# MLP of a hybrid decoder trunk: the low parts that GpSimd made are made by VectorE

## The chip, the cores and the metric

The kernel runs on one core of one Trainium2 chip. A core has five engines with a queue of instructions each: TensorE (PE in the profile; its weight loads are PEld), VectorE (DVE), ScalarE (ACT), GpSimd (POOL) and SyncE (SP), which here only issues DMAs. Each engine works its queue in order and waits for the others through semaphores. The metric is the time of one execution on the device, in microseconds (us); lower is better. Times given for a kernel are medians of several runs, and beside them stands one execution that was profiled.

## The reference

One decoder layer in float32 on 2048 tokens of width 1024: a mixer (retention and pooling), cross-attention into 256 memory tokens, and a gated MLP, each behind an RMSNorm and with a residual, and a last RMSNorm. The change lies in the MLP, whose inner width D_FF is 2816:

```python
def conv_glu_ffn(h, w_up, conv_w, conv_b, w_down):
    a = h @ w_up
    S = a.shape[1]
    a1 = jnp.pad(a, ((0, 0), (1, 0), (0, 0)))[:, :S]
    a2 = jnp.pad(a, ((0, 0), (2, 0), (0, 0)))[:, :S]
    c = conv_w[0] * a2 + conv_w[1] * a1 + conv_w[2] * a + conv_b
    gate, val = jnp.split(c, 2, axis=-1)
    return (jax.nn.silu(gate) * val) @ w_down
...
x = x + conv_glu_ffn(rmsnorm(x, ffn_norm_g[l]), ffn_w_up[l], ffn_conv_w[l],
                     ffn_conv_b[l], ffn_w_down[l])
return rmsnorm(x, final_norm_g)
```

## The kernel before

**Numbers in two parts.** Activations stand with features on the 128 partitions and tokens along the free axis. A float32 operand x of a matrix product is kept as a high part hi, x rounded to the type that TensorE multiplies at full rate (fp32r), and a low part lo = x - hi. A product is then three matmuls into one PSUM bank, hi by hi, hi by lo and lo by hi (`passes`, L241 to L243).

**Seven products for eight.** Each matrix product of the MLP is cut into 2 x 2 blocks, of the weights (two column blocks by two halves of the inner dimension) and of the tokens (two halves of 512 tokens by the same two halves), and done in seven block products in the manner of Strassen and Winograd. They need sums of weight blocks and of token blocks. Sums of weight blocks are made long before by accumulating DMAs and lie in DRAM (`Ud`, `Dd`). Sums of token blocks are made by GpSimd (`sums_of`, in four tensor operations on 128 x 512) and stored to DRAM (`Hd`, `Gd`) through SyncE's queue (`send`).

**Rounds.** The 2048 tokens are two batch halves b of 1024. `rounds` lists eight rounds: the up-projection of half 0 and of half 1, 22 members (`Up`) each, and then for each half the down-projection in three rounds of 4 members (`Down`), over 3, 4 and 4 tiles of the inner dimension. A member is one pair of column blocks of weights with its seven products i = 0 to 6; a product with n inner tiles is 3n matmuls, 12 in the up rounds. Up members run one by one, apart from the first two and the last two, which alternate product by product; down members alternate in pairs.

**Combined tokens.** A round needs 7n tiles of combined tokens, `right(i, j)`, each a high and a low part of 128 x 512 in the tensor G. `combining` makes one: a load from DRAM into a slot T (L948), the high part on ScalarE (L955; L953 for the negated product 2), the low part by `low`, or by one instruction on VectorE for product 2. Tiles for the next round are begun as soon as the last product of the running round that uses their place is done, so they come in a burst where two rounds meet.

**Weights.** For each product of a member the block is loaded into a slot R (L1000), ScalarE writes its high part (L1006) and `low` its low part into one of seven pair buffers, three in the tensor Q and four in G. They are made up to seven products ahead of TensorE.

**How a low part is made.** `low` (L934) has three ways: `""`, one subtraction on VectorE with both inputs in SBUF; `"copy"`, in which ScalarE first copies x to PSUM (tile `aux`, L940) and VectorE subtracts from there; and `"pool"`, the same subtraction on GpSimd. A member's `how` names one for each product: in `Up` products 2 and 6 go the pool way, in `Down` products 2 and 6 too. Of the combined tokens every fourth goes the pool way (`rd.shared`), in the second and third round every third, apart from product 2; the others of product 1 go the copy way. All tensor-tensor operations are recorded in one helper, `tt`, at L216, and all scalar-tensor-tensor ones in `stt`, at L225; so the profile tells them apart by engine and tiles: a subtraction into G or Q, from R (weights) or T, consts and state (tokens), is a low part.

**After a product.** `evac` of `Up` copies a product's bank into Z on ScalarE (L1052) or adds it there on VectorE (`Z<-Z,mm`); products 0, 2, 4 and 6 accumulate in one bank, so the evacuation of each must be done before the next of them starts, one product later. Then come the causal convolution, a scaled copy on ScalarE (L1069) and two steps on VectorE (`Z<-Z,vecs` of 1024 columns), SiLU on ScalarE (L1081), the gating product on VectorE (`Z<-Z` of 1024 columns), its store (L974), and for each second member the token sums for the down rounds. `evac` of `Down` adds or subtracts into Z. During the up rounds of half 0 the tokens of half 1 are normalised (VectorE, `T<-T,vecs`) and summed (GpSimd).

**What sets the order.** `run` walks over all products and writes each engine's instructions in program order: low parts of pairs just begun, the matmuls, the evacuation, then the next pairs and loads, then up to two steps of convolutions, then steps of combined tiles. A scheduler in the framework then moves instructions on each engine by its own estimate of times, within the dependences. SyncE's queue carries loads and stores of the MLP alike, in that order.

Of the kernel before, what the change touches and what calls it, by code (L numbers as in the profile page):

```python
# [8 lines left out]
F32 = mybir.dt.float32  # L9
# [3 lines left out]
ALU = mybir.AluOpType  # L13
# [106 lines left out]
def trunk(ctx, tc, xT, memT, pos, w_qkgu, w_v, wkv, wqT, wo, wout_r, wout_p, poolT, w_up, w_dn, vecs, consts, outT):  # L120
    nc = tc.nc
    pe, act, dve, pool, sp = nc.tensor, nc.scalar, nc.vector, nc.gpsimd, nc.sync
# [83 lines left out]
    def aux():  # L206
        if both[0] and next(turns_) % 3 == 2:
            return single()
        return auxp.tile([P, SUB], F32, tag="aux", name=nm("aux"))
# [5 lines left out]
    def tt(eng, out, a, b, op):  # L215
        return eng.tensor_tensor(out=out, in0=a, in1=b, op=op)  # L216
# [7 lines left out]
    def stt(out, a, s, b, op0=ALU.mult, op1=ALU.add):  # L224
        dve.scalar_tensor_tensor(out=out, in0=a, scalar=s, in1=b, op0=op0, op1=op1)  # L225
# [698 lines left out]
    class Round:  # L924


        def __init__(self, src, n, groups):
            self.src, self.n, self.groups = src, n, groups

            self.shared = 4  # L930

    def right(i, j, h):
        at = (4 * i + j) * T + h * SUB
        return G[:, at : at + SUB]  # L934

    def low(x, hi, lo, how):

        if how == "copy":
            t = aux()[:, : x.shape[-1]]
            act.activation(t, x, AF.Copy)  # L940
            x = t
        tt(pool if how == "pool" else dve, lo, x, hi.bitcast(F32), ALU.subtract)

    def combining(rd, i, j):

        r = TT.take()
        x = r.f[:, :SUB]
        sp.dma_start(x, rd.src(i, j))  # L948
        yield
        yield  # L950
        hi, lo = right(i, j, 0), right(i, j, 1)
        if i == 2:
            act.activation(hi, x, AF.Copy, scale=-1.0)  # L953
        else:
            act.activation(hi, x, AF.Copy)  # L955
        yield
        if i == 2:
            stt(lo, x, -1.0, hi.bitcast(F32), ALU.mult, ALU.subtract)
        else:
            low(x, hi, lo, "pool" if (i * rd.n + j) % rd.shared == rd.shared - 1 else "copy" if i == 1 else "")  # L960
        r.free()

    def sums_of(b11, b12, b21, b22, t):
# [20 lines left out]
    def combine(rd, i):  # L984
        in_turn(combining(rd, i, j) for j in range(rd.n))

    class Member:
# [21 lines left out]
        def low(self, i, hi, lo):  # L1009
            low(self.raw[i].f[:, : self.n * P], hi, lo, self.how[i])  # L1010
            self.raw.pop(i).free()
# [14 lines left out]
    class Up(Member):  # L1026


        def __init__(self, b, f):
            super().__init__((w_up[f], w_up[f + NF]), Ud[f], 0, 4)  # L1030
            self.b, self.f, self.how = b, f, ("", "copy", "pool", "", "copy", "", "pool")
            self.c = {}

        def bank(self, i, spare):
# [87 lines left out]
    class Down(Member):  # L1122
# [2 lines left out]

        def __init__(self, b, j, at, k0, halves):
            super().__init__((w_dn[2 * j], w_dn[2 * j + 1]), Dd[at, j], k0, halves)
            self.b, self.j, self.at, self.how = b, j, at, ("copy", "copy", "pool", "copy", "copy", "", "pool")

        def bank(self, i, spare):  # L1130
            return gathered(self, i, spare)
# [179 lines left out]
    def rounds():  # L1311
        out = []
        for b in range(NB):
            ups = [Up(b, f) for f in range(NF)]
            groups = [ups[:2]] + [[u] for u in ups[2:-2]] + [ups[-2:]]
            out.append(Round(lambda i, j, b=b: Hd[b, j, i], 4, groups))
        for b in range(NB):
            for at, (k0, n) in enumerate(ROUNDS):
                ms = [Down(b, j, at, k0, n) for j in range(KT // 2)]
                out.append(Round(lambda i, j, b=b, k0=k0: Gd[b, k0 // 2 + j, i], n, [ms[:2], ms[2:]]))  # L1320
        out[1].shared = out[2].shared = 3
        return out

    def run(rds):
# [45 lines left out]
        def begin():  # L1370
            rd, i, j, _, first = tiles.pop(0)
            live.append((first, combining(rd, i, j)))
            next(live[-1][1])
# [125 lines left out]
    for b in range(NB):  # L1499
# [56 lines left out]
        if b + 1 < NB:  # L1556
            nxt = [TT.take() for _ in range(NS)]
            got = fetch_x(b + 1, 0)
        else:
            rds = rounds()  # L1560
# [166 lines left out]
```

## Time and profile before

| | us |
|---|---|
| median of 3 runs | 2502.49 (2500.76 to 2505.65) |
| profiled execution, its own time | 2506.72 |
| its span, from the first to the last instruction | 2504.9 |

| engine | busy us of the span | share |
|---|---|---|
| TensorE | 2442.7 | 98% |
| VectorE | 1666.9 | 67% |
| ScalarE | 1216.1 | 49% |
| GpSimd | 652.4 | 26% |

The mean granted clock of TensorE is 0.992. How the page is read: a line of a group gives line, engine, operation, tiles (out<-in, buffer numbers left out), the form and the number of instructions; then their busy us and the mean ns of one; then the idle us of the engine just ahead of them and what ended most of it. Busy time of an engine that is not the bottleneck costs nothing by itself, and an average over the span hides stages with different limits, so the views are asked by stage.

### The profile page before, as it was taken

To read this page: it belongs to the slowest core of one execution; us is meant where nothing else is said; L and a number is where in the kernel's file an instruction comes from. 1 tells how busy PE (TensorE), PEld (TensorE's weight loads), DVE (VectorE), ACT (ScalarE), POOL (GpSimd) and SP (SyncE) were. 2 spreads that over 40 slices of the span, in tenths; PEclk is the share of its full clock that TensorE was granted. 3 is DMA by queue.
4 is the path that set the end of the run, shared out by engine and by line. 5 is a ranking of instruction groups with operands and counts; after the bars stand their busy time and mean duration, and the time that the engine had idled before them with its cause. 6 is when DMAs were issued, how large, how long until landed. Compare 5 with 4: busy or idle time off the path is not lost.

```text
span 2504.9 us, 33172 instructions
## 1 busy us (share of the span) xinstructions
PE 2442.7 (98%) x11390; PEld 2037.7 (81%) x11390; DVE 1666.9 (67%) x2574; ACT 1216.1 (49%) x2163; POOL 652.4 (26%) x579
## 2 busy tenths in 40 slices
PE   6999999999999999999999999999999999999997
PEld 6888887788788888888887888878888887888885
DVE  8646566564635675574678776886677586867875
ACT  6333423343321223434654555665555576666663
POOL 1010122100121120030237352553335154222322
PEclk9999999999999999999999999999999999999998
DMA  8363888715766764366567564755556468768951
GB/s 318 89 168 110 244 191 233 234 40 181 227 152 145 159 158 149 111 221 220 167 205 270 166 203 153 236 192 165 160 160 213 136 220 287 250 185 280 346 164 68
DMA packets 257177, 474.28 MB, mean 189 GB/s; under 512 B 26864, under 2 KB 56176, under 8 KB 257008
## 3 DMA queue, kind: packets, MB, share of 16 engines
q1 hardware_dynamic: 212336, 408.18, 49.0%
q0 software_dynamic: 19584, 34.61, 8.9%
q10 hardware_dynamic: 25088, 29.37, 3.4%
q8 instruction: 89, 1.46, 0.2%
q14 instruction: 80, 0.66, 0.1%
HBM read 370.87 MB, written 170.39 MB: 216 GB/s over the span
## 4 chain that ended last, share of the span: by engine, by line
PE 78%; DMA 8%; DVE 6%; issue 3%; POOL 2%; ACT 2%; SPq 0%; POOLq 0%; ACTq 0%; DVEq 0%
PE mm L241 25%; PE mm L242 24%; PE mm L243 24%; POOL T L216 1%; DVE Z L216 1%; DMA T<-Xd 1%; DVE Z L225 1%; DVE G L216 1%; DMA T<-xT 1%; DVE Q L216 1%; DVE T L216 1%; DMA T<-Gd 1%; POOL Z L216 1%; PE aux L749 1%; DMA R<-VWd 0%
## 5 line engine op out<-in xcount | busy, mean ns | idle before, releaser
L241 PE MATMUL mm<-G,Q 128*128 128x512 f32 (+1 forms) x1888 | 728.1, 386 | 21.8 <-ACT Q L233 11.1
L243 PE MATMUL mm<-G,Q 128*128 128x512 f32 (+1 forms) x1888 | 725.9, 385 | 4.4 <-DVE Q L216 4.2
L242 PE MATMUL mm<-G,Q 128*128 128x512 f32 (+1 forms) x1888 | 725.7, 385 | 0.7 <-DVE G L216 0.7
L241 PE MATMUL mm<-G 128*128 128x512 f32 (+1 forms) x1380 | 532.1, 387 | 10.0 <-DVE Z L216 6.3
L242 PE MATMUL mm<-G 128*128 128x512 f32 (+1 forms) x1380 | 531.7, 386 | 0.0
L243 PE MATMUL mm<-G 128*128 128x512 f32 (+1 forms) x1380 | 531.1, 385 | 0.0
L241 PEld LDWEIGHTS mm<-G,Q 128*128 128x128 f32 x1888 | 357.8, 190 | 91.1 <-ACT Q L233 11.8
L243 PEld LDWEIGHTS mm<-G,Q 128*128 128x128 f32 x1888 | 357.7, 190 | 74.3 <-DVE Q L216 5.9
L242 PEld LDWEIGHTS mm<-G,Q 128*128 128x128 f32 x1888 | 358.0, 190 | 69.4 <-DVE G L216 1.6
L225 DVE SCALAR_TENSOR_TENSOR Z<-Z,vecs 128x1024 f32<-128x1024 f32 x176 | 276.3, 1572 | 153.5 <-ACT Z L1069 145.3
L241 PEld LDWEIGHTS mm<-G 128*128 128x128 f32 x1380 | 260.4, 189 | 64.5 <-DVE Z L216 8.0
L243 PEld LDWEIGHTS mm<-G 128*128 128x128 f32 x1380 | 260.2, 189 | 51.8
L242 PEld LDWEIGHTS mm<-G 128*128 128x128 f32 x1380 | 260.1, 188 | 51.5
L1006 ACT ACTIVATE G<-R 128x512 fp32r<-128x512 f32 (+1 forms) x272 | 166.5, 615 | 197.8 <-PE mm L242 178.6
L216 DVE TENSOR_TENSOR Z<-Z,mm 128x512 f32<-128x512 f32 x284 | 192.8, 679 | 78.2 <-PE mm L243 78.0
L216 DVE TENSOR_TENSOR Q<-R,Q 128x512 fp32r<-128x512 f32 x199 | 148.6, 748 | 143.4 <-ACT Q L233 138.9
L216 POOL TENSOR_TENSOR G<-R,G 128x512 fp32r<-128x512 f32 (+1 forms) x100 | 141.9, 1420 | 376.2 <-ACT G L1006 290.9
L233 ACT ACTIVATE Q<-R 128x512 fp32r<-128x512 f32 x150 | 93.8, 627 | 234.8 <-PE mm L242 187.3
L1006 ACT ACTIVATE Q<-R 128x512 fp32r<-128x512 f32 (+1 forms) x204 | 125.0, 613 | 90.9 <-PE mm L242 73.5
L216 DVE TENSOR_TENSOR G<-R,G 128x512 fp32r<-128x512 f32 (+1 forms) x168 | 131.5, 794 | 46.7 <-ACT G L233 38.0
L216 DVE TENSOR_TENSOR G<-T,G 128x512 fp32r<-128x512 f32 (+1 forms) x168 | 125.4, 758 | 53.9 <-ACT G L955 40.7
L940 ACT ACTIVATE aux<-R 128x512 f32<-128x512 f32 (+1 forms) x184 | 105.8, 576 | 95.8 <-DVE Q L216 52.9
(222 smaller groups left out, 2911.4 us busy)
## 6 DMA issues: line engine op xcount, KB each, us to landing
R<-Ud SPq DMA_DIRECT2D x176, 256.0 KB, 2.7
T<-Gd SPq DMA_DIRECT2D x168, 256.0 KB, 4.1
R<-w_up SPq DMA_DIRECT2D x132, 256.0 KB, 3.1
Gd<-Z SPq DMA_DIRECT2D x110, 256.0 KB, 2.4
Ud<-w_up SPq DMA_DIRECT2D x88, 256.0 KB, 5.9
R<-w_qkgu SPq DMA_DIRECT2D x32, 512.0 KB, 4.4
R<-Dd SPq DMA_DIRECT2D x64, 256.0 KB, 4.0
Gd<-T SPq DMA_DIRECT2D x56, 256.0 KB, 3.1
```

The lines of the kernel that those rows point to most:

```text
L216: return eng.tensor_tensor(out=out, in0=a, in1=b, op=op)
L225: dve.scalar_tensor_tensor(out=out, in0=a, scalar=s, in1=b, op0=op0, op1=op1)
L233: act.activation(hi, src, AF.Copy)
L241: pe.matmul(ps, lh, rh, start=start, stop=False, skip_group_check=more)
L242: pe.matmul(ps, lh, rl, start=False, stop=False, skip_group_check=more)
L243: pe.matmul(ps, ll, rh, start=False, stop=stop, skip_group_check=more)
L749: pe.matmul(col(self.kv, c), col(self.kn.f, c), self.ch(v, c, h * T), start=True, stop=True)
L940: act.activation(t, x, AF.Copy)
L1006: act.activation(p2[:, 0, :w], self.raw[i].f[:, :w], AF.Copy)
```

## The change

No low part goes to GpSimd any more. In `low` the engine is always VectorE; in the two `how` tuples `"pool"` becomes `""`; in `combining` the tiles that went to GpSimd go the way of the others of their product, which is the copy way for product 1 and the plain way else; the attribute `shared`, which chose them, goes. GpSimd keeps the token sums, the small copies of the convolution's halo, and the DMAs that it issues.

```diff
@@ class Round
             self.src, self.n, self.groups = src, n, groups
 
-            self.shared = 4
-
@@ def low(x, hi, lo, how)
-        tt(pool if how == "pool" else dve, lo, x, hi.bitcast(F32), ALU.subtract)
+        tt(dve, lo, x, hi.bitcast(F32), ALU.subtract)
@@ def combining(rd, i, j)
         if i == 2:
             stt(lo, x, -1.0, hi.bitcast(F32), ALU.mult, ALU.subtract)
         else:
-            low(x, hi, lo, "pool" if (i * rd.n + j) % rd.shared == rd.shared - 1 else "copy" if i == 1 else "")
+            low(x, hi, lo, "copy" if i == 1 else "")
@@ class Up
-            self.b, self.f, self.how = b, f, ("", "copy", "pool", "", "copy", "", "pool")
+            self.b, self.f, self.how = b, f, ("", "copy", "", "", "copy", "", "")
@@ class Down
-            self.b, self.j, self.at, self.how = b, j, at, ("copy", "copy", "pool", "copy", "copy", "", "pool")
+            self.b, self.j, self.at, self.how = b, j, at, ("copy", "copy", "", "copy", "copy", "", "")
@@ def rounds()
-        out[1].shared = out[2].shared = 3
         return out
```

## The prediction

> **What bounds the kernel now.** I read the busy time by stage first, then who ends TensorE's waits, then the stretches in which those waits lie. The first rows give, for a stretch, its length and the busy us of TensorE, its weight loads, VectorE, ScalarE and GpSimd, then TensorE's granted clock and the share and GB/s of the DMAs.
> ```profile
> 1204.00:2485.00 1281.00, 1268.56 (x5585) 1047.71 (x5583) 930.66 (x1112) 778.86 (x1266) 481.28 (x369) 1.00 0.61 201
> 2485.00:2505.00 20.00, 3.69 (x17) 2.74 (x17) 11.21 (x25) 2.23 (x4) 8.65 (x7) 0.55 0.56 210
> ```
> The MLP runs from 1204 to 2485 us, and every edit but a few early combined tokens lies in it. TensorE is busy 1268.6 of 1281.0 us, so 12.4 us are open to any change of the other engines. One matmul takes 1268.56 / 5585 = 0.227 us, a product of twelve 2.72 us. VectorE is busy 73%, GpSimd 38%.
>
> TensorE's waits from 1170 us on (what waited, for what: us in all, times, longest):
> ```profile
> PE aux L1255 <- DVE Q L216: 7.7, 3, 6.6
> PE mm L241 <- DVE Z L216: 6.3, 4, 3.2
> PE mm L241 <- ACT G L955: 3.3, 1, 3.3
> PE mm L241 <- ACT Z L1052: 2.1, 1, 2.1
> ```
> The first is the final norm, after the last product, which the change doesn't touch. The others, 11.7 us, are all that can be won as waits. They are not evenly spread: they lie where a round ends or the second batch half is normalised. A stall has a tail:
> ```profile
> 1625.00:1650.00 25.00, 25.00 (x111) 20.37 (x110) 23.91 (x22) 20.10 (x32) 16.61 (x14) 1.00 0.46 154
> 1650.00:1675.00 25.00, 22.91 (x95) 18.44 (x94) 19.52 (x22) 14.10 (x22) 17.33 (x12) 0.93 0.67 232
> ```
> Ahead of the 2.1 us wait VectorE is nearly full (23.91 of 25 us); behind it the granted clock averages 0.93, which costs (1 - 0.93) x 25 = 1.75 us more.
>
> **What the change moves.** These GpSimd groups (mean ns after the comma) hold the low parts, into G and Q; T<-T is the sums that stay:
> ```profile
> L216 POOL TENSOR_TENSOR G<-R,G 128x512 fp32r<-128x512 f32 x84 | 123.3, 1470 | 324.8 <-ACT G L1006 269.7 <-PE mm L242 32.0 <-DMA T<-Gd 11.9
> L216 POOL TENSOR_TENSOR T<-T 128x512 f32<-128x512 f32 x41 | 67.8, 1655 | 9.2 <-DVE T L225 6.8 <-DMA Hd<-T 0.6
> L216 POOL TENSOR_TENSOR G<-T,G 128x512 fp32r<-128x512 f32 x38 | 58.3, 1534 | 113.7 <-ACT G L955 79.6 <-DVE Z L216 13.3 <-PE mm L243 10.4
> L216 POOL TENSOR_TENSOR Q<-R,Q 128x512 fp32r<-128x512 f32 x36 | 54.8, 1523 | 66.5 <-ACT Q L1006 66.5
> ```
> By the code, 44 up members and 24 down members give two low parts of weights each, 136, and the eight rounds give 47 of combined tokens: 183 in all, of which the three groups hold 158; the others are 384 wide or lie in other tiles. Eight of the 47 (product 1) now go the copy way, the other 175 straight to VectorE. No DMA is added; the order of loads and stores on SyncE shifts a little, as do VectorE's instructions.
>
> What one costs VectorE, and what its GpSimd form costs VectorE already:
> ```profile
> L225 DVE SCALAR_TENSOR_TENSOR Z<-Z,vecs 128x1024 f32<-128x1024 f32 x176 | 276.3, 1572 | 153.5 <-ACT Z L1069 145.3 <-issue 6.9
> ...
> L216 DVE TENSOR_TENSOR G<-R,G 128x512 fp32r<-128x512 f32 x98 | 82.9, 847 | 3.4 <-ACT G L1006 3.2
> L216 DVE TENSOR_TENSOR G<-T,G 128x512 fp32r<-128x512 f32 x86 | 71.7, 850 | 28.3 <-ACT G L955 28.1
> L216 DVE TENSOR_TENSOR Q<-aux,Q 128x512 fp32r<-128x512 f32 x95 | 65.1, 686 | 38.7 <-ACT Q L1006 36.2 <-PE mm L243 1.9 <-ACT aux L940 0.7
> ...
> L216 DVE TENSOR_TENSOR Q<-R,Q 128x512 fp32r<-128x512 f32 x47 | 41.9, 891 | 3.9 <-ACT Q L1006 3.9
> ```
> The same subtraction takes 686 ns with one input in PSUM and 847 to 891 ns on average with both in SBUF. The timelines show why. First a stretch where rounds meet, VectorE (start, us), then GpSimd's first and last low part of the four in it:
> ```profile
> 1634.06 1.79 DVE L216 TENSOR_TENSOR G<-consts,G 128x512 fp32r<-128x512 f32 x1
> 1635.77 1.27 DVE L225 SCALAR_TENSOR_TENSOR Z<-Z,vecs 128x1024 f32<-128x1024 f32 x1
> 1636.97 1.78 DVE L216 TENSOR_TENSOR G<-T,G 128x512 fp32r<-128x512 f32 x1
> 1638.68 2.31 DVE L225 SCALAR_TENSOR_TENSOR Z<-Z,vecs 128x1024 f32<-128x1024 f32 x1
> 1640.91 0.68 DVE L216 TENSOR_TENSOR G<-T,G 128x512 fp32r<-128x512 f32 x1
> 1641.51 1.27 DVE L225 SCALAR_TENSOR_TENSOR Z<-Z,vecs 128x1024 f32<-128x1024 f32 x1
> 1642.71 1.78 DVE L216 TENSOR_TENSOR G<-R,G 128x512 fp32r<-128x512 f32 x1
> ...
> 1646.21 1.21 DVE L216 TENSOR_TENSOR Z<-Z 128x1024 f32<-128x1024 f32 x1
> ```
> ```profile
> 1632.95 2.34 POOL L216 TENSOR_TENSOR G<-R,G 128x512 fp32r<-128x512 f32 x1
> ...
> 1641.59 2.35 POOL L216 TENSOR_TENSOR G<-T,G 128x512 fp32r<-128x512 f32 x1
> ```
> A subtraction is 0.68 us alone and 1.78 beside a low part on GpSimd; the convolution step 1.27 and 2.31. Each of the four low parts here holds VectorE up by 1.04 to 1.11 us, 4.35 in all. On VectorE it costs 0.60 us, the distance of two starts (1640.91 to 1641.51). So the stretch gives back 4.35 - 4 x 0.60 = 1.95 us, in the place where VectorE is late.
>
> A steady up tile, in contrast (VectorE, then GpSimd):
> ```profile
> 1411.52 3.52 DVE L225 SCALAR_TENSOR_TENSOR Z<-Z,vecs 128x1024 f32<-128x1024 f32 x2 [4.30 <-ACT Z L1069]
> ```
> ```profile
> 1409.80 1.29 POOL L216 TENSOR_TENSOR G<-R,G 128x512 fp32r<-128x512 f32 x1 [5.81 <-ACT G L1006]
> 1412.51 1.44 POOL L216 TENSOR_TENSOR Q<-R,Q 128x512 fp32r<-128x512 f32 x1 [1.41 <-ACT Q L1006]
> ```
> The first low part falls into 4.30 us in which VectorE idles: it costs nothing while that cover lasts, 0.60 us without. The second stretches two steps to 3.52 us where two alone are 2 x 1.27 = 2.54: its 0.60 replaces 0.98. So steady tiles, without a TensorE wait now, stay so, and I put them at 0.
>
> Over the MLP, the four slowed groups exceed their bare forms by 176 x (1.572 - 1.27) + 98 x 0.161 + 86 x 0.164 + 47 x 0.205 = 93 us; low parts are 236 of the 304 us of the four GpSimd groups quoted, and as other sums share the blame I take six tenths, 55 us. Against 183 x 0.69 = 126 us added, VectorE ends some 70 us busier, 78% of the MLP. GpSimd falls by at least 236 us. Both are totals of engines that don't set the end.
>
> The Trainium skill ("Perfetto Trace Analysis", Optimizing Scalar/DVE Operations) says that a saturated VectorE may be helped by giving work to GpSimd, but adds that the two share an SBUF read port, so that it might not help. Taken by its first half alone, the four low parts would make the saturated stretch 4 x 0.60 = 2.4 us longer and the 2.1 us wait 4.5; the row above, 1.78 against 0.68, is for the second half, and the sum goes by the row.
>
> Now the path. How VectorE reaches the 2.1 us wait, in the chain of waits:
> ```profile
> 1646.21 1.22 DVE Z L216
> ...
> 1650.11 3.91 DMA Gd<-T
> ```
> The gating product at 1646.21 releases a store on SyncE's queue; weight loads queue behind it, ScalarE's copy behind them, TensorE's bank behind that. With that product 1.95 us earlier, 0.15 of 2.1 us is left and, I take it, no slow clock: -1.95 - 1.75 = **-3.7 us** (bounds: 0, if a weight load is late for another reason, to -3.85).
>
> The 3.2 us wait, which ends at 1367 us, has a low part on its chain:
> ```profile
> 1355.88 2.25 POOL G L216
> ...
> 1366.96 0.53 PE mm L241
> ```
> It precedes a sum, the reuse of a buffer, a load and VectorE's norm multiply. Gone from GpSimd it saves 2.25; two low parts put before the same multiply on VectorE cost 1.2: **-1.0 us** (bounds -2.25 to +1.2).
>
> The rest of the 6.3 us and the 3.3 us wait hang on sums that stay: 0 (bounds: all gone, -7; or 0.60 for each of the three low parts before each of the three waits, +5.4). The eight copies stand on ScalarE at about the 576 ns of the page's copy group: 4.6 us on an engine busy 779 of 1281, 0 on the path, 4.6 if none is hidden.
>
> Sum: -3.7 - 1.0 = -4.7 us: the profiled execution's 2506.72 becomes 2502.0. It ran 4.2 us above the median of the runs; on the median, 2502.49 - 4.7 = **2498 us**. About 0.2%, 5 us, is what a measurement of this kernel tells from no change, so this lies on that border.
>
> **The rivals.** *Relief everywhere.* GpSimd's sums no longer stand behind low parts, their stores free SyncE sooner, and all three stalls dissolve: 11.7 us of waits and three tails, 17 us at most; two thirds of it, -11, give 2491. For it: sums and low parts alternate on GpSimd around 1356 us. Against: the sums meet more VectorE subtractions now, and GpSimd's own 1.29 becomes 2.35 beside them.
>
> *Nothing moves.* The stalls hang on loads and sums; the 55 us of relief fall where VectorE idles anyway: 2502. For it: VectorE idles 350 us of the MLP. Against: the full stretch at 1625.
>
> *VectorE in order, slower.* A low part on GpSimd that waits for its high part delays only low parts; on VectorE the evacuations queue behind it. An up member's fifth product must leave its bank within the sixth, 2.72 us, of which 0.68 is the evacuation: at 2.0 us of lateness TensorE stops. The changed program's order on VectorE puts both low parts ahead of the convolution steps that precede the evacuations. If a weight lands late where VectorE is full, at round ends and in the norm of the second half, such stalls come anew: 6.3 / 4 = 1.6 us plus a tail of 1.75, 3.3 each; three make +10, 2512, five +17. For it: VectorE-ended waits are already the commonest kind, and 183 more instructions in one in-order queue make it more exposed. Against: the low parts that VectorE makes today wait for ScalarE little (3.4 and 3.9 us idle in two groups). It decides once two or more new stalls appear.
>
> **How the numbers follow.** Forecast 0.46 (own range 2494 to 2502, not quite half of it beyond 0.2%), relief everywhere 0.12, nothing 0.08, slower 0.34. Faster: 0.22 + 0.12 = 0.34; same: 0.24 + 0.08 = 0.32; slower 0.34. The range, 2489 to 2514, takes in two thirds of all stalls gone below and three to four new ones above; it leaves out some 0.04 and 0.14.
>
> **What would show it.** Right: no L216 low part into G or Q on GpSimd; VectorE's subtractions with two SBUF inputs near 0.75 us, its convolution step near 1.4 us; no wait of TensorE on L1052 near 1650 us and a clock of 1.00 there. Wrong: TensorE waits for DVE Z L216 more than four times or over 6.3 us, with evacuations behind a low part that stood waiting for ScalarE; or subtractions that stay at 0.85 us, since then it was the sums that slowed them.

## The result

| | before | after |
|---|---|---|
| median of 22 runs each, us | 2502.98 (2496.32 to 2507.45) | 2497.32 (2490.56 to 2503.83) |
| ratio to before, 95% interval | | 0.998 (0.9972 to 0.9987) |
| first profiled execution, its own time | 2506.72 | 2497.77 |
| second profiled execution, its own time | 2496.92 | 2500.59 |

The change makes the kernel 0.2% faster, 3.3 to 7.0 us by the interval. The forecast was 2498 us. Another 12 runs of after gave 2498.39 us, a ratio of 0.9974 (0.9961 to 0.9986). The second row of profiles is a warning: the two profiled executions of before lie 10 us apart, and the 22 runs of after spread over 13 us, so the runs carry the verdict and the profiles only say where time lies.

How much of the first pair's 8.9 us belongs to the change? The line that copies products into Z (L1052, in after L1050) starts with the first product of the MLP. These are its instructions up to 1230 us (engine, operation, tiles and count, then shortest, median and longest ns, first and last start), in before and in a second execution of before:

```profile
L1052 ACT ACTIVATE Z<-mm x6: 577/581/588, 1205.6 to 1218.6; 128x512 f32<-128x512 f32 x6
```
```profile
L1052 ACT ACTIVATE Z<-mm x7: 578/581/590, 1198.1 to 1230.0; 128x512 f32<-128x512 f32 x7
```

The MLP begins 7.5 us apart in two executions of the same kernel. TensorE's stalls in it come again at the same places, though not with the same lengths (below). In the two of after the first copy starts at 1199.0 and 1202.5 us. From that first copy to the end of the span (2504.9, 2495.2, 2496.0 and 2498.8 us) it takes 1299.3 and 1297.1 us before, 1297.0 and 1296.3 after. I use this length below for every kernel. Of the first pair's difference, 6.6 us arose ahead of the MLP and 2.3 in it.

**The profile after.** The MLP by its windows (columns as before); first the stretch 1204 to 2480 in before, then in after, where the next two rows are the meeting of the up rounds, 6 us earlier than in before:

```profile
1204.00:2480.00 1276.00, 1264.27 (x5567) 1044.52 (x5566) 926.45 (x1098) 777.30 (x1263) 481.28 (x369) 1.00 0.61 202
```
```profile
1204.00:2480.00 1276.00, 1262.67 (x5575) 1042.83 (x5573) 960.01 (x1284) 778.99 (x1266) 226.57 (x194) 1.00 0.61 201
...
1619.00:1644.00 25.00, 25.00 (x112) 20.66 (x111) 25.00 (x35) 20.83 (x34) 7.68 (x8) 1.00 0.72 240
1644.00:1669.00 25.00, 25.00 (x112) 20.71 (x111) 23.96 (x27) 14.19 (x23) 15.25 (x12) 1.00 0.73 246
```

VectorE has 186 instructions more, 183 of them the low parts, and is busy only 33.6 us longer; GpSimd falls by 254.7 us. At the round meeting VectorE is full, 25.00 of 25 us, and TensorE waits for nothing: 25.00 in both windows, clock 1.00. That is the reading to learn: a full helper engine that delays nothing.

VectorE's groups that the prediction named, in after:

```profile
L225 DVE SCALAR_TENSOR_TENSOR Z<-Z,vecs 128x1024 f32<-128x1024 f32 x176 | 244.7, 1393 | 55.8 <-ACT Z L1067 50.2 <-issue 2.7 <-DMA R<-Ud 1.1
...
L216 DVE TENSOR_TENSOR G<-R,G 128x512 fp32r<-128x512 f32 x180 | 139.1, 774 | 79.2 <-ACT G L1004 76.2 <-DMA R<-Ud 2.9
L216 DVE TENSOR_TENSOR G<-T,G 128x512 fp32r<-128x512 f32 x112 | 76.5, 702 | 26.4 <-ACT G L953 26.2
```

The convolution step fell from 1572 to 1393 ns, the subtractions into G from 847 and 850 to 774 and 702. But look at the idle time ahead of G<-R: 3.4 us before, 79.2 now. VectorE now stands waiting for ScalarE's high part, which GpSimd did in its stead. It doesn't show in the end, because in before it idled 145.3 us for ScalarE ahead of the convolution step, and now 50.2: by its size mostly the same idle time under another name.

TensorE's waits from 1170 us on, after, then the second execution of before and of after (the final norm's row left out):

```profile
PE mm L241 <- DVE Z L216: 7.7, 5, 4.8
PE mm L243 <- DVE G L216: 2.3, 1, 2.3
PE aux L241 <- ACT Q L1004: 0.6, 1, 0.6
```
```profile
PE mm L241 <- DVE Z L216: 5.5, 4, 2.3
PE mm L241 <- ACT G L955: 3.0, 1, 3.0
PE mm L241 <- ACT Z L1052: 1.2, 1, 1.2
```
```profile
PE mm L241 <- DVE Z L216: 7.7, 3, 4.7
PE mm L241 <- ACT Z L1050: 0.6, 1, 0.6
```

The waits are 11.7 and 9.7 us before, 10.6 and 8.3 after. The waits on L1052 and L955 are gone or small; the row of DVE Z has grown from 6.3 and 5.5 to 7.7 and 7.7. A wait for a low part (DVE G L216) is new in the first execution of after; it was expected again in the second, and isn't there. So it isn't one gain but two gains and a loss.

### The profile page after: what moved, and what is told of

It is laid out like the page before. It is cut to its first block, busy times and chain, and to the rows that moved or that the text cites. A ratio compares the mean times of both kernels' runs of the same rounds, so it can differ in the third digit from the quotient of the medians.

```text
span 2496.0 us, 33121 instructions
## 1 busy us (share of the span) xinstructions
PE 2439.3 (98%) x11390; PEld 2035.1 (82%) x11390; DVE 1699.9 (68%) x2757; ACT 1220.0 (49%) x2171; POOL 387.9 (16%) x396
## 5 line engine op out<-in xcount | busy, mean ns | idle before, releaser
L225 DVE SCALAR_TENSOR_TENSOR Z<-Z,vecs 128x1024 f32<-128x1024 f32 x176 | 244.7, 1393 | 55.8 <-ACT Z L1067 50.2
L216 DVE TENSOR_TENSOR G<-R,G 128x512 fp32r<-128x512 f32 (+1 forms) x268 | 196.7, 741 | 115.4 <-ACT G L1004 76.8
L216 DVE TENSOR_TENSOR Q<-R,Q 128x512 fp32r<-128x512 f32 x235 | 174.0, 742 | 148.1 <-ACT Q L233 138.4
L216 DVE TENSOR_TENSOR Z<-Z,mm 128x512 f32<-128x512 f32 x284 | 193.3, 681 | 88.3 <-PE mm L243 87.8
L216 DVE TENSOR_TENSOR G<-T,G 128x512 fp32r<-128x512 f32 (+1 forms) x201 | 134.8, 685 | 51.1 <-ACT G L953 37.7
L1067 ACT ACTIVATE Z<-Z,vecs 128x1024 f32<-128x1024 f32 x88 | 109.3, 1242 | 51.6 <-DVE Z L216 50.0
L216 DVE TENSOR_TENSOR T<-T 128x512 f32<-128x512 f32 (+4 forms) x161 | 109.6, 689 | 35.1 <-POOL T L630 17.6
```

The source lines that it names most:

```text
L1067: act.activation(self.c[g].f, a[:, 2:], AF.Identity, bias=cb[:, f : f + 1], scale=cw[2][:, f : f + 1])
```

## The experiments

In the expectations "before" and "after" are the two kernels; ratios are to the kernel before, run beside each.

**1. Weights alone.** Tokens' low parts stay on GpSimd.

```diff
@@ class Up
-            ... self.how = b, f, ("", "copy", "pool", "", "copy", "", "pool")
+            ... self.how = b, f, ("", "copy", "", "", "copy", "", "")
@@ class Down
-            ... self.how = b, j, at, ("copy", "copy", "pool", "copy", "copy", "", "pool")
+            ... self.how = b, j, at, ("copy", "copy", "", "copy", "copy", "", "")
```

> Only the low parts of weights (136) go to VectorE; every fourth or third combined token stays on GpSimd. Theory A (the gain comes from VectorE being held up beside GpSimd's low parts where rounds meet): two of the four low parts near 1640 us are weights', so VectorE gains about 1 us there; the 2.1 us wait of TensorE on L1052 near 1650 us shrinks to about 1 us or goes. Theory B (in-order VectorE loses in the norm of the second half: low parts of weights stand behind VectorE's waits for loads): TensorE's waits near 1335 to 1365 us come to 7 to 9 us as in the changed kernel, against 5.8 us before. Both together: a time 0 to 3 us under the kernel before. Rival (the gain is a free GpSimd, whose sums come earlier): most of the gain is kept, 4 to 5 us under.

Measured: 2502.55 us, ratio 0.9991 (0.9979 to 1.0002), within the expected 0 to 3 us. The wait on L1052 is gone. In the stretch of the norm (1300 to 1380 us) TensorE waits 6.6 us, against 5.8 and 4.4 in before, and one of these waits is for a low part (DVE G L216, 2.3 us).

**2. Tokens alone.** Weights' low parts stay on GpSimd.

```diff
@@ def combining
-            low(x, hi, lo, "pool" if (i * rd.n + j) % rd.shared == rd.shared - 1 else "copy" if i == 1 else "")
+            low(x, hi, lo, "copy" if i == 1 else "")
```

> Only the low parts of combined tokens (47) go to VectorE; weights' products 2 and 6 stay on GpSimd. Theory A: about 1 us of relief near 1640 us, so the 2.1 us wait there shrinks to about 1 us or goes. Theory B: the waits near 1335 to 1365 us stay at about 5.8 us, as no weights' low part moved. Both: 1 to 4 us under the kernel before. Rival (a free GpSimd): little is freed, 47 of 183, so 0 to 1.5 us under.

Measured: 2499.38 us, ratio 0.9976 (0.9965 to 0.9988): 6 us, more than the 1 to 4 expected. TensorE's waits with tokens alone (the final norm's row left out):

```profile
PE mm L241 <- DVE Z L216: 6.5, 3, 3.0
PE mm L241 <- ACT G L955: 2.1, 1, 2.1
```

47 low parts give a gain as large as all 183 do; the 136 of weights, three quarters of the work that moved, give at most 0.2%, and the interval reaches zero. The new wait for a low part comes with the weights, where it comes at all: not one is in this view.

**3. None at all.** The 183 low parts are left out, on both engines: what the work is worth at most. The reference's low-order terms are then missing in those operands.

```diff
@@ def low
-        tt(dve, lo, x, hi.bitcast(F32), ALU.subtract)
+        if how != "pool":
+            tt(dve, lo, x, hi.bitcast(F32), ALU.subtract)
```

> Leaves out the 183 low parts that GpSimd made before: nobody computes them. VectorE has neither the 0.6 us of each nor the hold-up beside GpSimd. Theory A: the waits near 1650 and 2075 us are gone as in the changed kernel or shorter. Theory B: without low parts behind VectorE's waits for loads the waits near 1335 to 1365 us fall under the 5.8 us of before. Both: 6 to 10 us under the kernel before. If it is only as fast as the changed kernel, low parts on VectorE cost nothing and theory B falls.

Measured: 2493.4 us, ratio 0.996 (0.9948 to 0.9972), at the upper end of the expected 6 to 10 us. TensorE's waits in the MLP fall to 4.8 us, all of them in the norm's stretch. Its MLP by the window:

```profile
1204.00:2480.00 1276.00, 1263.25 (x5580) 1044.88 (x5578) 854.09 (x1122) 776.95 (x1259) 235.49 (x196) 0.99 0.62 202
```

This splits VectorE's account. Taking the low parts off GpSimd relieves VectorE by 926.45 - 854.09 = 72.4 us; making them there costs 960.01 - 854.09 = 105.9 us, 0.58 each. In time, the low parts cost some 0.4% of the kernel on GpSimd and 0.2% on VectorE.

**4. The norm's stretch undone.** After, with products 2 and 6 of members 5 to 8 of the first up round back on GpSimd: eight low parts, those made while the second half is normalised (`low` sends `"pool"` to GpSimd again).

```diff
@@ class Up
-            ... self.how = b, f, ("", "copy", "", "", "copy", "", "")
+            ... self.how = b, f, ("", "copy", "pool", "", "copy", "", "pool") if b == 0 and 5 <= f <= 8 else ("", "copy", "", "", "copy", "", "")
```

> The changed kernel, but up members 5 to 8 of half 0 (the stretch in which the tokens of half 1 are normalised) keep products 2 and 6 on GpSimd: 8 low parts. Theory B: the 2.3 us wait on a low part (DVE G L216) is gone and the waits near 1335 to 1365 us fall from 7.9 us to 5.8 us or less; the rest stays as in the changed kernel: 2 to 5 us under the changed kernel, 7 to 10 us under the kernel before. Rival (the waits there are VectorE's total load, or hang on loads from DRAM): 7 to 9 us of waits stay, and the time is that of the changed kernel within 1 us.

Measured: 2497.35 us, ratio 0.9979 (0.9966 to 0.9992): in time not to be told from after, where 2 to 5 us less were expected. Its profile has no wait for DVE G L216, but neither has the second one of after. Its other waits are 8.1 us for DVE Z L216, longest 3.9, and 0.3 elsewhere; 6.0 of them lie in the norm's stretch, against 7.9 and 6.7 in after. So the rival of this experiment, waits that stay and a time like after's, came nearer. The MLP, 2495.3 - 1200.0 = 1295.3 us, is about a microsecond under after's two, which the runs can't show.

**5. GpSimd busy, but with few columns.** After, with two GpSimd operations of 64 columns that read the high part into a scratch, beside some 172 of the low parts that it made (those keep the mark `"pool"`, which now only adds the two).

```diff
@@ def low
         tt(dve, lo, x, hi.bitcast(F32), ALU.subtract)
+        if how == "pool":
+            for _ in range(2):
+                tt(pool, scr, hi[:, :64].bitcast(F32), hi[:, :64].bitcast(F32), ALU.subtract)
```

> The changed kernel, and beside it GpSimd works twice for each of some 172 low parts on 64 columns of the high part, into a scratch that nobody reads: no work is taken from VectorE, only GpSimd's reading of SBUF comes back. Theory A (VectorE is held up beside GpSimd): VectorE's subtractions with two SBUF inputs go from about 0.75 us up to 0.85 or more and its convolution step from 1.39 to 1.5 or more; TensorE's waits in the MLP grow from about 10 to 14 us or more; the time is 3 to 10 us over the changed kernel. Rival (what counts is only that GpSimd's sums don't queue behind low parts): these queue behind the copies as well, so waits grow too, but VectorE's durations stay within 0.03 us. If neither moves, the gain was VectorE's order alone.

Measured: 2499.45 us, ratio 0.9981 (0.9969 to 0.9993), as after. GpSimd's new operations, and VectorE's steps beside them:

```profile
L217 POOL TENSOR_TENSOR phalo<-G 128x64 f32<-128x64 f32 x268 | 156.9, 585 | 541.7 <-ACT G L1008 467.6 <-ACT G L957 61.6
```
```profile
L226 DVE SCALAR_TENSOR_TENSOR Z<-Z,vecs 128x1024 f32<-128x1024 f32 x176 | 244.6, 1394 | 55.5 <-ACT Z L1071 45.9 <-issue 7.2 <-DMA R<-Ud 1.1
```

GpSimd is busy 414 us from 1204 to 2480, against 481 in before and 227 in after, and VectorE's convolution step stays at 1394 ns; VectorE is busy 967.5 us, 8 more than in after. So GpSimd's busy time alone hardly slows VectorE. The hold-up wasn't put back, so neither the 3 to 10 us that it was expected to cost nor the theory was tested.

**6. Other queue for the stores.** After, with the stores of GpSimd's token sums of the norm (and the convolved ones) issued from GpSimd's queue instead of SyncE's, so that loads don't stand behind them.

```diff
-    def send(to, aps):
+    def send(to, aps, by=sp):
...
-            sp.dma_start(to[i], a)
+            by.dma_start(to[i], a)
```

> The changed kernel, but the stores of token sums that GpSimd has made are issued by GpSimd itself and no longer by SyncE. Theory C (the stalls left at 143 to 167 us come from SyncE's queue: loads of tokens stand behind stores that wait for GpSimd's sums, and VectorE, in order, stands at the multiply that waits for those loads, with low parts and evacuations behind it): VectorE's idle time ahead of that multiply (T<-T,vecs) falls by half or more, TensorE's waits there from about 8 to 3 us or less; 3 to 8 us under the changed kernel. Rival (the stalls there are VectorE's load beside GpSimd's sums): they stay within 1.5 us, and so does the time; if issuing costs GpSimd more than its idle time gives, the time is over the changed kernel.

Measured: 2504.17 us, ratio 0.9994 (0.9983 to 1.0005): the gain is lost, where 3 to 8 us more were expected. The waits in the MLP are now many and small, 11.7 us in six rows, the largest 3.8 for DVE Z L216 and 3.3 for ACT Z L1050. The row of DVE Z halves, but others take its place. The remedy fails, and what it was meant to show (that those stores are what the norm's loads wait for) stays unproved.

**7 and 8. One meeting at a time.** The kernel before, with only the 7 low parts of the second up round's tokens on VectorE, and with only the 34 of the down rounds' tokens.

```diff
-        out[1].shared = out[2].shared = 3
+        out[1].shared, out[2].shared = 99, 3
```
```diff
-        out[1].shared = out[2].shared = 3
+        out[1].shared = 3
+        for rd in out[2:]:
+            rd.shared = 99
```

> The kernel before, with only the 7 low parts of the second up round's combined tokens moved to VectorE (one more goes the copy way where it is of product 1); all others stay on GpSimd. Theory (each round meeting is relieved by its own burst): the wait on ScalarE's copy into Z some 455 us into the MLP (2.1 and 1.2 us in the two profiles of before) falls under 0.7 us, the wait some 878 us in stays at about 3 us, ratio to before 0.9985 to 0.9995, 1 to 4 us. Rival (the first meeting is worth nothing; the gain is all at the start of the down rounds): the 455 us wait may go, but the time stays, 0.9995 to 1.0005.

> The kernel before, with only the 34 low parts of the six down rounds' combined tokens moved to VectorE. Theory (each round meeting is relieved by its own burst): the wait some 878 us into the MLP falls from about 3 us to 2 or less and the one at 455 us stays at 1 to 2 us; ratio 0.998 to 0.9995, 1 to 5 us. Rival, the recorded prediction's own book-keeping (the down rounds hang on sums that stay, the gain is at 455 us): both waits stay and the time is that of before, 0.9995 to 1.0005. If 7 and 34 low parts together give clearly less than the 47 did (0.9976), part of that gain was the first round's or the state of the runs.

Measured: 2500.71 us, ratio 0.9989 (0.9978 to 1.0), and 2499.54 us, 0.999 (0.9981 to 1.0). The waits of the one, then of the other:

```profile
PE mm L241 <- DVE Z L216: 6.3, 5, 2.3
PE mm L241 <- ACT G L955: 3.5, 1, 3.5
```
```profile
PE mm L241 <- DVE Z L216: 6.4, 3, 3.5
PE mm L241 <- ACT G L955: 1.8, 1, 1.8
PE mm L241 <- ACT Z L1052: 1.5, 1, 1.5
```

Each set mends its own meeting and leaves the other's: with the 7 the wait on L1052 is gone and the one on L955 stays at 3.5 us; with the 34 the one on L955 falls to 1.8 and that on L1052 stays. The two ratios together, 0.0011 + 0.0010, are about the 0.0024 of experiment 2; each alone has an interval that touches 1, so the sizes are rough, while the waits tell the theories apart. With the weights alone the wait on L955 is gone too, but others take its place: from 2000 to 2150 us TensorE waits 4.8 us there, 3.8 in before and 1.8 with the 34.

**9 and 10. The hold-up put back in full.** First the base, after with one buffer (`state`) less among the slots T. Then the same with one GpSimd subtraction of full width beside some 172 low parts, which reads the high part and writes to that buffer. VectorE's own work is that of after.

```diff
-    for a in (state.rearrange("p h n -> p (h n)"), cs_t[:, P + 1 : P + 1 + SUB]):
+    for a in (cs_t[:, P + 1 : P + 1 + SUB],):
```
```diff
@@ def low
         tt(dve, lo, x, hi.bitcast(F32), ALU.subtract)
+        if how == "pool":
+            w = x.shape[-1]
+            tt(pool, scr[:, :w], hi.bitcast(F32), hi.bitcast(F32), ALU.subtract)
```

> The kernel after with one slot T less in the MLP (the buffer state isn't given to the slots), as the base for the next kernel. Expected of both theories: as after, ratio to before 0.9975 to 0.999, VectorE's convolution step near 1.39 us, its subtraction into G from R near 0.77. If the slot matters, the waits in the norm of the second half grow and the ratio is over 0.999.

> The kernel before this one (after with one slot T less), and beside each of some 172 low parts that GpSimd made before, GpSimd does one subtraction of the same width that reads the high part twice and writes to a buffer that nobody reads; so the work is left on VectorE and GpSimd's SBUF traffic is put back. Theory A (the hold-up of two engines that read SBUF at once, by columns read): VectorE's convolution step goes back from 1.39 to 1.5 to 1.6 us, the subtraction into G from R from 0.77 to 0.84 or more, VectorE's busy time in the MLP rises by 40 to 90 us, and the time by 3 to 10 us over that kernel (ratio to before 0.999 to 1.003). Theory B (what helped is the place in GpSimd's and VectorE's queues, not the hold-up): those durations stay within 0.04 us of 1.39 and 0.77, and the time within 1.5 us.

Measured: 2500.32 us, ratio 0.9993 (0.9983 to 1.0004), and 2519.65 us, 1.006 (1.0044 to 1.0077). VectorE's groups without and with GpSimd's extra work:

```profile
L225 DVE SCALAR_TENSOR_TENSOR Z<-Z,vecs 128x1024 f32<-128x1024 f32 x176 | 248.5, 1414 | 57.9 <-ACT Z L1067 53.8 <-issue 2.7 <-DMA T<-Gd 1.0
...
L216 DVE TENSOR_TENSOR G<-R,G 128x512 fp32r<-128x512 f32 x180 | 140.4, 780 | 77.4 <-ACT G L1004 76.9 <-DMA R<-Ud 0.4
...
L216 DVE TENSOR_TENSOR Q<-R,Q 128x512 fp32r<-128x512 f32 x82 | 66.9, 815 | 8.7 <-ACT Q L1004 8.7
```
```profile
L226 DVE SCALAR_TENSOR_TENSOR Z<-Z,vecs 128x1024 f32<-128x1024 f32 x176 | 262.3, 1494 | 56.6 <-ACT Z L1071 47.8 <-issue 4.6 <-POOL state L217 1.7
...
L217 DVE TENSOR_TENSOR G<-R,G 128x512 fp32r<-128x512 f32 x180 | 157.8, 877 | 70.1 <-ACT G L1008 70.0
...
L217 DVE TENSOR_TENSOR Q<-R,Q 128x512 fp32r<-128x512 f32 x82 | 90.3, 1101 | 7.4 <-ACT Q L1008 5.9 <-DMA R<-Ud 1.6
```

The same instructions of VectorE take 13.8 + 17.4 + 23.4 = 54.6 us longer, in these three groups, with GpSimd's subtractions beside them; from 1204 to 2480 us VectorE is busy 1034.7 us in place of 966.8. The time rises by 19.3 us, twice what was expected at most. TensorE's waits without and with it (the final norm's left out):

```profile
PE mm L241 <- ACT G L953: 4.0, 3, 3.3
PE mm L241 <- DVE Z L216: 2.4, 2, 1.6
PE mm L241 <- ACT Z L1050: 1.9, 1, 1.9
PE mm L243 <- DVE Q L216: 1.2, 1, 1.2
```
```profile
PE mm L242 <- DVE Z L217: 5.7, 7, 1.5
PE mm L244 <- DVE Q L217: 5.2, 3, 2.3
PE mm L242 <- ACT G L957: 4.6, 3, 2.7
PE mm L242 <- ACT Z L1054: 3.6, 1, 3.6
PE mm L244 <- DVE G L217: 3.5, 1, 3.5
```

From 9.5 us they rise to 22.6, in 15 places; the rest of the 19.3 is not in this view. VectorE with all the low parts has room for the work, and none for the hold-up as well. One thing is mixed in: a high part's place is also held until GpSimd has read it, so a part of the 19 us may be that and not VectorE's slower steps; this was not taken apart. The base kernel shows that a slot T is worth something too: a wait of 3.3 us on L953 is there that after doesn't have, and its ratio is over the expected range.

## Why the prediction was right, and where its steps were not

**VectorE's totals.** Added 126 us, relief 55, some 70 busier: measured 106, 72 and 34 (experiment 3 against before and after). Both terms missed in the same direction, against the change. A low part cost 0.58 us and not 0.69, which was the busy time of one instruction; the distance of starts, 0.60 in the prediction's own row, was the better price. And the share of the hold-up put down to low parts, six tenths, should have been nearly eight (72 of 93), which is just their share of the busy time quoted, 236 of 304: the discount for the other sums had no row behind it. The sign and the engine were right, and experiment 10 shows the cause of the relief: put GpSimd's subtractions back and VectorE's steps slow down by 55 us in three groups.

**The round meeting, -3.7.** The place and the sign were right, the size hung on one execution, and the path held only in part. The wait on L1052 is gone with the 7 low parts alone, with the weights alone and with the tokens alone; in after it is gone in one execution and 0.6 us in the other. Alone (experiment 7) it is worth some 2.8 us, by an interval from nothing to 5.5. Of the 3.7, 1.75 was the slow clock behind the wait, and that didn't come again: in the second execution of before the wait is 1.2 us and the clock from 1640 to 1665 us is 1.00. With the clock, the two executions lose 3.9 and 1.2 us here.

The path was to be an earlier gating product. With the 7 alone (start, us; in after it starts at 1644.72):

```profile
1641.42 1.21 DVE L216 TENSOR_TENSOR Z<-Z 128x1024 f32<-128x1024 f32 x1
```

From the first copy of the MLP (1202.3 and 1199.0) these are 439.1 and 445.7 us, against 1646.21 - 1205.6 = 440.6 in before. So the seven alone bring it 1.5 us earlier, near the prediction's 1.95; the whole change brings it 5.1 us later, and still TensorE doesn't wait. SyncE's queue tells why, in before and then with the 7 alone:

```profile
1647.45 1.10 SPq L974 DMA_DIRECT2D Gd<-Z  x2
1648.64 0.41 SPq L1000 DMA_DIRECT2D R<-w_up  x1
1649.14 0.88 SPq L1000 DMA_DIRECT2D R<-Ud  x2
```
```profile
1641.52 0.33 SPq L1000 DMA_DIRECT2D R<-w_up  x1
1641.95 0.86 SPq L1000 DMA_DIRECT2D R<-Ud  x2
1642.90 0.85 SPq L974 DMA_DIRECT2D Gd<-Z  x2
```

In before the loads of weights stand behind the product's store, as the prediction has it. With the 7 alone the scheduler has put them ahead of it, and they are issued 3.8 us earlier (439.2 for 443.0 us after the first copy), more than the product's 1.5. They stand ahead of the store in both executions of after and in experiments 1 and 2 too, and behind it in both of before and in experiment 8, where the wait stays. Only experiment 3 shows the predicted path by itself: the store is still ahead of the loads, the product comes 5.4 us earlier than in before, and the wait is gone, while TensorE's product ahead of it begins as in before (445.4 us after the first copy, 445.5 in experiments 3 and 7). Whether 1.95 us would have done it without the new order is not shown.

ScalarE's order differs as well, in before and in after (the rows between, its other copies, left out):

```profile
1645.80 0.60 ACT L1052 ACTIVATE Z<-mm 128x512 f32<-128x512 f32 x1
...
1653.79 0.60 ACT L940 ACTIVATE aux<-R 128x512 f32<-128x512 f32 x1 [1.75 <-DMA R<-Ud]
1654.33 0.58 ACT L1052 ACTIVATE Z<-mm 128x512 f32<-128x512 f32 x1
```
```profile
1643.11 0.60 ACT L1050 ACTIVATE Z<-mm 128x512 f32<-128x512 f32 x1
...
1645.88 0.58 ACT L1050 ACTIVATE Z<-mm 128x512 f32<-128x512 f32 x1
1646.56 0.60 ACT L938 ACTIVATE aux<-R 128x512 f32<-128x512 f32 x1
```

The first row is the last copy into Z before the wait (440.2 and 444.1 us after the first copy; TensorE's next product, in `aux`, begins at 445.4 and 449.1, the 3.7 us of difference being lost in the norm's stretch). In before the next evacuation stands behind an `aux` copy that waits for its weights, and follows after 8.53 us. In after it stands ahead of that copy, and follows after 2.77 us. In the full change the new order did what the earlier product was to do. The prediction said that the order of loads and stores shifts a little, and did not price it.

**The norm of the second half, -1.0.** This step failed, in sign: TensorE's waits from 1300 to 1380 us are 5.8 and 4.4 us in the two executions of before, 7.9 and 6.7 in those of after. The prediction saw a low part on the chain of the 3.2 us wait and took it off; what came in its place is the slower rival's mechanism, in the rival's place. VectorE in after (in brackets the idle time before, and who ended it), then TensorE:

```profile
1346.66 0.75 DVE L225 SCALAR_TENSOR_TENSOR T<-T,vecs 128x512 f32<-128x512 f32 x1 [5.23 <-DMA T<-Xd]
1347.33 0.68 DVE L216 TENSOR_TENSOR G<-R,G 128x512 fp32r<-128x512 f32 x1
1350.48 0.75 DVE L225 SCALAR_TENSOR_TENSOR T<-T,vecs 128x512 f32<-128x512 f32 x1 [2.48 <-DMA T<-Xd]
...
1356.28 1.57 DVE L216 TENSOR_TENSOR G<-R,G 128x512 fp32r<-128x512 f32 x1
```
```profile
1357.91 0.51 PE L243 MATMUL mm<-G 128*128 128x512 f32 x1 [2.34 <-DVE G L216]
```

VectorE stands 5.23 and 2.48 us at two norm multiplies whose loads aren't there, with low parts queued behind them; TensorE reaches the operand of the last one and waits 2.34 us. On GpSimd those low parts would not have stood in VectorE's queue. In before the same multiplies wait 0.82 and 0.70 us, and the two ahead of them, which wait for nothing in after, 2.83. The long wait at the first of the two, 5.2 to 5.4 us, is in both executions of after and in experiments 1 and 5; it is 0.8 to 1.1 us in both of before and in experiments 2, 3, 4, 7 and 8, where the weights' low parts of this stretch are on GpSimd or left out. So the weights' low parts on VectorE bring it (with a slot T less, experiment 9, the order is another). Why the loads come later with them stays open: GpSimd's sums and their stores on SyncE's queue are ahead of them, but experiment 6, which took the stores off that queue, did not help. And the runs of experiment 4, which undid this stretch, don't show the loss, so its size rests on profiles alone.

**The rest, 0.** Wrong as well, the other way: the 3.3 us wait on L955 was said to hang on sums that stay. Experiment 8 takes nearly half of it away by moving low parts of the down rounds' tokens alone, and is worth 2.5 us by an interval from nothing to 4.8. It was a second round meeting, with a burst of low parts as at the first, and the prediction gave it no term; by which path the low parts held it up was not followed. The steady up tiles at 0 stand: from 180 to 430 and from 470 to 850 us behind the first copy TensorE is busy throughout, in both executions of both kernels. The eight copies were not tested by themselves.

So -4.7 against a measured -5.0 (by the ratio; 5.7 by the medians) is partly luck: one gain too many at the norm, one too few at the down rounds, and at the first meeting a size that only one execution showed, won in the full change by another order. What stays open is the sum: the two pairs of profiles show the MLP shorter by 1.6 us on average (1298.2 and 1296.6), the runs show 3.3 to 7.0, and two executions of one kernel differ by more than this gap.

**The rivals.** The signs named for being right came: subtractions at 0.77 and 0.70 us, the convolution step at 1.39, no wait on L1052 in the first execution and a clock of 1.00 there. Of *VectorE in order*, the stall behind a late load came once, and it needed two to decide. Its mark, waits on DVE Z L216 over 6.3 us or more than four times, was met in its numbers (7.7 us, five times) in a kernel that got faster, and what VectorE stood waiting for was a load and not ScalarE: the numbers were too weak a mark, since they didn't count what went elsewhere. *Relief everywhere* was right about the second meeting and wrong about the norm. *Nothing moves* falls with experiments 2, 3 and 10.

## What to carry to other kernels

When two engines slow each other, price the work by what it costs both: here the low parts on GpSimd cost VectorE, in hold-up, two thirds of what making them itself costs it (72 of 106 us). Look for the place where the bursts are: 47 low parts at the round meetings were worth as much as all 183, and the other 136, most of them in steady tiles, 0.2% at most. Read the order of the queues again after a change: a scheduler that moves instructions can matter as much as the work that was moved. Size a term that hangs on one wait from more than one execution. And before work is put into an in-order queue, look for waits on loads in that queue near it, because everything that is put there waits with them.

## What the runs showed of the hardware

In these runs the hold-up between the two engines goes with the columns that GpSimd works on and not with how long the profile shows it busy. Some 340 operations of 64 columns, 0.55 to 0.59 us each, left VectorE's convolution step at 1394 ns and its busy time from 1204 to 2480 us within 8 us of after's; some 172 of full width (512 columns, 16 of them 384; 1.0 to 1.4 us each) took the step from 1414 to 1494, the subtraction into Q from 815 to 1101 and the busy time up by 68 us. Each of these operations both read and wrote SBUF, so the runs don't tell reading from writing. The Trainium skill ("SBUF — State Buffer", SBUF: two separate sides) says that of a VectorE instruction with two SBUF inputs and a GpSimd instruction that reads SBUF, the one that starts first has the shared ports for the whole instruction and the other is fully blocked. The rows of full width agree that they hold each other up; for the 64-column ones a lock held over the whole 0.55 us that the profile shows would, it seems, have cost more than the 8 us seen, so the lock may be held for the reading alone. That last step is argued and not measured.
